# Four pairs of column groups of two up projections with tokens on partitions, most of their pairs of rows with seven block products, and the residual restored earlier

## The chip, the cores and the metric

The kernel runs on one core of a Trainium2 chip. Times are device microseconds (us) of one execution. Engines work in parallel, each in its own order of instructions: TensorE (PE) multiplies, VectorE (DVE) and ScalarE (ACT) work on elements, GpSimd (POOL) and SyncE (SP) only issue transfers here. Semaphores hold an instruction back until what it reads is there and what it overwrites is free.

## The reference

Two layers work on 256 tokens of width 2048, in fp32. Layer 0 mixes tokens with a gated MLP, layer 1 with latent attention. After each mixer comes the part that is changed here, a gated MLP with a causal convolution of width 3 between its two projections (D_FF = 5504, 43 blocks of 128 features; `w_up` is 2048 x 11008, `w_down` 5504 x 2048, `m` is the mixer's result):

```python
def conv_ffn(x, w_up, conv_w, conv_b, w_down):
    h = x @ w_up
    C = h.shape[-1]
    h = lax.conv_general_dilated(h, conv_w[:, None, :], window_strides=(1,),
                                 padding=[(CONV_W - 1, 0)],
                                 dimension_numbers=('NWC', 'WIO', 'NWC'),
                                 feature_group_count=C) + conv_b
    a, g = jnp.split(h, 2, axis=-1)
    return (jax.nn.silu(g) * a) @ w_down
...
        x = layer_norm(ALPHA * x + m, ln_mix_g[i], ln_mix_b[i])
        f = conv_ffn(x, ffn_w_up[i], ffn_conv_w[i], ffn_conv_b[i], ffn_w_down[i])
        x = layer_norm(ALPHA * x + f, ln_ffn_g[i], ln_ffn_b[i])
```

## The kernel before, in words

**Weights.** All weights stream once from memory in chunks of mostly 1 MB (128 x 2048 fp32). SP loads each into one of 3 "raw" slots. fp32 is emulated with two parts of fewer bits: ACT casts the chunk to a high part `wh` (L125), DVE subtracts that from it to get a low part `wl` (L128), each into one of 14 "big" slots. PE then multiplies three times with parts of the activations, high by high, low by high, high by low (all recorded on L230, the helper `mm`). `Feed.next` hands out chunk i, after it has issued splits up to chunk i+2 and loads up to i+4.

**Two kinds of product.** A chunk "wide" holds two k-rows of 128 by 1024 columns. With the two blocks of 128 tokens that is a product of 2x2 by 2x2 blocks: `Banks.eight` makes its eight block products, 24 matmuls of 128x512. `Banks.seven` makes it with seven products of sums of blocks, 21 matmuls; each seven chunk has its weights' sums made by DVE (`_seven`, L135: one add of 1024 elements, two of 512) and split in turn (`th` by ACT, `tl` by DVE, beside `wh` and `wl` of 1536), takes five big slots, and needs sums of the activations, made by DVE and split as well. The eight accumulators fill all eight PSUM banks; `rest` then combines four of them, and four more adds close the group. The gMLP's two projections and the down projections work like this.

**The up projection** works differently. Its 86 chunks per layer (144 to 229 in layer 0, 314 to 399 in layer 1) make groups `gi` of four chunks, 22 in all; group 0 is done with tokens on partitions at the boundary before, while the norm is still being applied. In groups 1 to 21, `prod_a` puts features on partitions: weights stand still and 512 columns move (256 tokens, high and low parts side by side), then 256 for the low part of the weights. So a group has 64 matmuls of 128x512 and 64 of 128x256 into four banks, two blocks of 128 features for `a` and two for `g`. `pair` ends a group: for each block `sum_halves` (L386 ACT copy `lo`, L388 DVE add `h`), the convolution (ACT, then two DVE scalar_tensor_tensor, L908 and L910), `silu` on ACT, and the gate's multiply (`act`, L925, DVE).

**Beside it** run three other things. `restore(f)` (L652, L653) brings back the residual, f = 0 to 3, with 4 DVE operations of 512 each and two row transfers by SP, after groups 2 to 5; `park(b)` then stores the residual by POOL after groups 4 and 6. `park_all` works on eight seven-chunks of the down projection ahead of time, 32 steps a layer, of which the groups from 2 on take up to two each: POOL loads `praw`, ACT and DVE split it and its sums (L152, L166, L167), POOL stores the four parts (L157), and they are fetched (`fwh`, `fwl`, `fth`, `ftl`, L187) when the down projection is within five chunks of their use. `acts.make` makes the first activation sums of the down projection in groups 19 and 20.

**Order.** Python code issues operations in program order, but a scheduler at build time sets the order of instructions on each engine, by what it holds ready first; on the chip each engine keeps that order.

Of the kernel before, what the change touches and what calls it, by code (L numbers as in the profile page):

```python
# [8 lines left out]
F32 = mybir.dt.float32  # L9
F32R = mybir.dt.float32r  # L10
# [5 lines left out]
P = 128  # L16
# [34 lines left out]

U_PAIRS = [[0, 1, 5, 7, 2, 6, 3, 4]] + [[0, 1, 2, 5, 3, 7, 4, 6]] * 5
U_SEVEN = [(2, 3)] + [(2, 3, 4)] * 4 + [(2, 3)]

T1, T2 = 6, 5
SLOTS = {"big": 14, "raw": 3, "side": 6}
# [15 lines left out]
def plan(n_k):  # L72

    return [[(int(t[:-1]), KINDS[t[-1]]) for t in line.split()] for line in PLAN[n_k]]
# [135 lines left out]
def trunk(ctx: ExitStack, tc: tile.TileContext, x, xT, gm_in, gm_wout, ffn_up, ffn_dn,  # L210
# [12 lines left out]
    def slot(shape, name, dt=F32, tag="big"):  # L223
        return big.tile(shape, dt, tag=tag, name=name, bufs=SLOTS[tag])
# [30 lines left out]
    def back(w, n_k):  # L255

        for hf, units in enumerate(plan(n_k)):
            c = slice(hf * 1024, (hf + 1) * 1024)
            for u, kind in units:
                if 2 * u + 1 == n_k:  # L260
                    chunks.append((w[2 * u, :, c], 1024, kind))
                    continue
                if kind == "parked":
                    parked.append(len(chunks))
                chunks.append((w[2 * u : 2 * u + 2, :, c].rearrange("k p c -> p k c"), 2048, kind))

    back(gm_wout, NF_GM)
    chunks += [(ffn_up[0, i], 2048, "") for i in range(n_up)]
    back(ffn_dn[0], NF_FF)
    chunks += [(ml_q[i], 2048, "") for i in range(4)]  # L270
    chunks += [(ml_kv[i], 3 * KVR, "") for i in range(5)] + [(ml_kv[5, :, 0:KVR], KVR, "")]
    chunks += [(ml_b[i], 2048, "") for i in range(ml_b.shape[0])]
    chunks += [(ml_out[i], 2048, "") for i in range(ml_out.shape[0])]
    chunks += [(ffn_up[1, i], 2048, "") for i in range(n_up)]
    back(ffn_dn[1], NF_FF)


# [18 lines left out]
    def combine(name, o, k1, k2):  # L296


        t = tp.tile([P, 4, P], F32, tag="t2", name=f"xs{name}", bufs=T2)
        turn(t, k1, k2)  # L300
        o = o.rearrange("p (h s c) -> p h s c", h=2, s=4)
        nc.scalar.copy(o[:, 0], t)
        nc.vector.tensor_tensor(o[:, 1], t, o[:, 0].bitcast(F32), ALU.subtract)
        return [(o[:, 0, i], o[:, 1, i]) for i in (1, 2, 0, 3)]
# [556 lines left out]
    def park_all(until):  # L861

        for i in [i for i in parked if feed.used < i < until]:
            yield from feed.park(i)
            yield
# [48 lines left out]
    def ffn(layer, ln, acc, end, last):  # L914
        act = [None] * 6
        acts = Acts(act, f"dn{layer}", NF_FF)

        def pair(a, acc_a, acc_g):
            if act[a // 8] is None:
                act[a // 8] = slot([P, 8, S], f"act{layer}_{a // 8}", tag="side" if a // 8 > 3 else "big")  # L920
            ca = conv(layer, a, acc_a, f"{layer}a{a}")
            cg = conv(layer, NF_FF + a, acc_g, f"{layer}g{a}")
            s = tp.tile([P, S], F32, tag="t1", name=f"s{layer}_{a}", bufs=T1)
            nc.scalar.activation(s, cg, AF.Silu)
            nc.vector.tensor_tensor(act[a // 8][:, a % 8, :], s, ca, ALU.mult)  # L925

        hb, ht = [], [None, None]

        def after(b, step, acc):
            if step == 0:  # L930
                ht[b] = tp.tile([P, 512], F32, tag="t2", name=f"upt{layer}_{b}", bufs=T2)
                nc.scalar.copy(ht[b], acc)
                return
            if b == 0:
                hb.extend(bank(f"uph{layer}_{f}") for f in range(2))
            for f in range(4):
                o = (f % 2) * S + b * P
                nc.tensor.transpose(hb[f // 2][:, o : o + P], ht[b][:, f * P : (f + 1) * P], ident)

        boundary(ln, acc, end, f"upf{layer}_", after)  # L940
        xhl, old = ln.new, ln
        jobs = park_all(feed.used + 2 * n_up)
        for gi in range(1, 22):
            nt, nk = (4, 4) if gi < 21 else (2, 8)
            acc = [bank(f"up{layer}_{gi}_{f}") for f in range(nt)]
            for c in range(KD // nk):
                hi, lo = feed.next()
                prod_a(acc, xhl, range(nk * c, nk * c + nk), hi, lo)
                if gi > 1 and c in (1, 2) and gi + c > 3:
                    next(jobs, None)  # L950
                if (gi, c) in FIRST:
                    acts.make(*plan(NF_FF)[0][FIRST.index((gi, c))])
                if gi == 1 and c == 0:
                    after(1, 1, None)
                    for f in range(2):
                        pair(f, hb[0][:, f * S : (f + 1) * S], hb[1][:, f * S : (f + 1) * S])
            for f in range(nt // 2):
                pair(2 * gi + f, acc[f], acc[nt // 2 + f])
            if 1 < gi < 6:
                old.restore(gi - 2)  # L960
            if gi in (4, 6):
                old.park(gi // 2 - 2)
        ln = Norm(2 * layer + 1, {}, old.put_away, last)
        return (ln, *down(NF_FF, act, f"dn{layer}", ln, acts, 4 if last else SKEW))

# [386 lines left out]
```

## Time and profile before

| what | us |
|---|---|
| median of 3 runs | 2465.73 |
| lowest and highest run | 2465.49, 2466.3 |
| profiled execution, first to last instruction (span) | 2464.6 |
| PE busy in it | 2458.1 (100%) |
| DVE busy in it | 2054.7 (83%) |
| ACT busy in it | 1459.3 (59%) |
| mean granted TensorE clock | 1.000 |

The profile records one execution; its own time is the span of 2464.6 us, and the median of the runs is 1.1 us above it. In a row such as `L128 DVE TENSOR_TENSOR wl<-raw,wh 128x1024 ... x420 | 504.1, 1220 | 86.0 <-ACT wh L125 65.3`, L128 is the line, then come engine and operation, output and inputs by the program's names, size, count, busy time in us, mean in ns of one, and the idle time of the engine right before such instructions with what ended most of it. PEld is PE's loading of weights, which goes on beside its multiplying.

### The profile page before, as it was taken

Reading aid. Unit: us, or ns where it says so; the run is one execution under the profiler, and the core shown is the slowest. Engines: PE = TensorE matmul, PEld = TensorE weight load, DVE = VectorE, ACT = ScalarE, POOL = GpSimd, SP = SyncE. Lnnn points to the kernel's source line nnn. Section 1 sums busy time; section 2 is a strip of 40 time slices with the busy share of each in tenths; the row PEclk is TensorE's granted clock in tenths of the full one; section 3 lists DMA queues with packets and bytes.
Section 4 is the critical chain, followed back from the end, with each engine's and each line's share of the span. In section 5 each row is a group of like instructions: output and inputs, shape, how many; then the busy total and the mean of one; then the engine's idle time right before and its main releaser. Section 6 shows DMA issues by size and latency. Waiting matters only on the chain. (4 is left out here: it accounts for less than half of the span.)

```text
span 2464.6 us, 32483 instructions
## 1 busy us (share of the span) xinstructions
PE 2458.1 (100%) x12494; PEld 2091.3 (85%) x12494; DVE 2054.7 (83%) x2734; ACT 1459.3 (59%) x1967; POOL 104.2 (4%) x202
## 2 busy tenths in 40 slices
PE   9999999999999999999999999999999999999999
PEld 7888888888888888888888888988888888888887
DVE  7999999989897788778777997867598787878798
ACT  6666665566565666656554566665565665555453
POOL 0000000000000000000001000000000000000000
PEclk9999999999999999999999999999999999999999
DMA  7555666656665778778868885544478787777885
GB/s 291 202 208 205 226 204 202 205 188 205 222 212 198 241 282 314 300 279 300 322 218 318 301 301 182 184 170 156 172 269 309 275 305 304 295 265 278 299 324 201
DMA packets 116428, 611.94 MB, mean 248 GB/s; under 512 B 10648, under 2 KB 10912, under 8 KB 75184
## 3 DMA queue, kind: packets, MB, share of 16 engines
q1 hardware_dynamic: 90128, 462.47, 52.9%
q0 software_dynamic: 26144, 147.39, 15.8%
q8 instruction: 98, 1.61, 0.3%
q14 instruction: 58, 0.48, 0.1%
HBM read 544.75 MB, written 65.06 MB: 247 GB/s over the span
## 5 line engine op out<-in xcount | busy, mean ns | idle before, releaser
L128 DVE TENSOR_TENSOR wl<-raw,wh 128x1024 fp32r<-128x1024 f32 (+4 forms) x645 | 958.4, 1501 | 169.5 <-ACT wh L125 124.0
L125 ACT CAST wh<-raw 128x1024 fp32r<-128x1024 f32 (+4 forms) x645 | 809.0, 1278 | 356.8 <-PE up L230 80.7
L230 PE MATMUL up<-xhl,wh 128*128 128x512 f32 x2624 | 611.4, 390 | 0.0
L230 PEld LDWEIGHTS up<-xhl,wh 128*128 128x128 f32 x2624 | 487.4, 188 | 97.8
L230 PEld LDWEIGHTS up<-xhl,wl 128*128 128x128 f32 x2624 | 325.8, 192 | 6.4
L230 PE MATMUL up<-xhl,wl 128*128 128x256 f32 x2624 | 328.1, 283 | 0.0
L125 ACT CAST th<-ts 128x1536 fp32r<-128x1536 f32 (+1 forms) x138 | 142.5, 1052 | 110.9 <-DVE ts L135 80.3
L230 PE MATMUL ub<-wh,xhl 128*128 128x512 f32 x576 | 179.5, 393 | 0.0
L128 DVE TENSOR_TENSOR tl<-ts,th 128x1536 fp32r<-128x1536 f32 (+1 forms) x138 | 163.2, 1221 | 10.4 <-PE dn_p L230 3.4
L230 PEld LDWEIGHTS ub<-wh,xhl 128*128 128x128 f32 x576 | 108.1, 188 | 24.2 <-issue 1.9
L230 PE MATMUL ub<-wl,xhl 128*128 128x512 f32 x288 | 112.1, 389 | 0.0
L135 DVE TENSOR_TENSOR ts<-ts,raw 128x512 f32<-128x512 f32 x138 | 95.1, 689 | 1.4
L135 DVE TENSOR_TENSOR ts<-raw 128x1024 f32<-128x1024 f32 x69 | 84.3, 1221 | 6.1 <-PE ub L230 3.8
L230 PE MATMUL mo<-wh,oT 128*128 128x512 f32 x256 | 82.5, 401 | 0.0
L230 PE MATMUL v_q<-wh,xhl 128*128 128x512 f32 x224 | 70.7, 391 | 0.3 <-ACT wh L125 0.3
L230 PEld LDWEIGHTS ub<-wl,xhl 128*128 128x128 f32 x288 | 54.1, 188 | 11.3
L230 PE MATMUL v_p<-wh,xhl 128*128 128x512 f32 x192 | 59.9, 389 | 0.0
L230 PEld LDWEIGHTS mo<-wh,oT 128*128 128x128 f32 x256 | 45.5, 189 | 7.1
L230 PEld LDWEIGHTS v_q<-wh,xhl 128*128 128x128 f32 x224 | 42.0, 188 | 10.5 <-ACT wh L125 1.9
L230 PE MATMUL mo<-wl,oT 128*128 128x512 f32 x128 | 50.1, 391 | 0.0
L724 ACT ACTIVATE lny<-lnt,lncol 128x128 f32<-128x128 f32 x96 | 36.6, 472 | 15.6 <-PE lnt L720 15.5
L388 DVE TENSOR_TENSOR h_0a<-up,lo_0a 128x256 f32<-128x256 f32 x41 | 17.2, 421 | 33.0 <-ACT lo_0a L386 33.0
(1838 smaller groups left out, 4338.4 us busy)
## 6 DMA issues: line engine op xcount, KB each, us to landing
raw<-in_ffn_up_dram SPq DMA_DIRECT2D x172, 1024.0 KB, 7.0
raw<-in_gm_in_dram SPq DMA_DIRECT2D x93, 1024.0 KB, 5.3
raw<-in_ffn_dn_dram SPq DMA_DIRECT2D x68, 1024.0 KB, 7.2
raw<-in_gm_wout_dram SPq DMA_DIRECT2D x48, 1024.0 KB, 5.3
praw<-in_ffn_dn_dram POOLq DMA_DIRECT2D x16, 1024.0 KB, 13.9
keptth<-pth POOLq DMA_DIRECT2D x16, 1024.0 KB, 8.1
kepttl<-ptl POOLq DMA_DIRECT2D x16, 1024.0 KB, 8.8
fth<-keptth POOLq DMA_DIRECT2D x16, 1024.0 KB, 9.4
```

The source lines that it names most:

```text
L125: cast = self.nc.scalar.copy(hi, raw)
L128: self.nc.vector.tensor_tensor(lo, raw, hi.bitcast(F32), ALU.subtract)
L135: add = lambda o, a, b: self.nc.vector.tensor_tensor(o, a, b, ALU.add)
L230: recent[0] = nc.tensor.matmul(o, l, r, start=start, stop=stop, skip_group_check=True)
L388: nc.vector.tensor_tensor(h, acc[:, 0:S], lo, ALU.add)
L724: nc.scalar.activation(y[:, j], t[:, j * P : (j + 1) * P], AF.Identity, bias=lncol[:, o : o + 1], scale=lncol[:, g : g + 1])
```

## The change

Groups 4 and 5 of each layer together, and groups 7 and 8, become a `token_group`: eight chunks, each a pair of k-rows by 512 columns of group gi and 512 of group gi+1, with tokens on partitions and all eight banks. Of the eight pairs of k, five (2, 3, 4, 5, 7) use seven products and three use eight. The activation sums for the five pairs are made in groups 2 and 3 (`sum_acts`: an add of 512, four of 128, a cast by ACT, a subtraction of 512). The result has tokens on partitions, so 16 transposes (`turn_group`) in the first chunk of the next group turn it, and `gate_group` runs `pair` on it in that group's next two chunks; there `sum_halves` is not needed, because high and low are already added. All four restores now follow groups 1 and 2, and the residual is parked after groups 2 and 3. A token group takes two parking steps, where the two groups that it replaces took four. The number of chunks and of bytes stays the same, and lines below the new code have higher numbers (L128 is L132 now, L157 L161, L187 L191, L388 L405); a token group's chunks are read as two pieces of 1024 columns instead of one of 2048.

**DVE, splitting chunks 161 and 162 of layer 0** (`wl`, `wh`, `raw`: parts of the chunk in the name; `ts`, `tl`: sums and their low part; `praw`: a parked chunk; `h_0a`, `c_0`, `act0`: the gate's tiles). Before:

```order
L128 TENSOR_TENSOR wl161_6634<-raw161_6547,wh161_6633 128x1024
L910 SCALAR_TENSOR_TENSOR c_0g5_6482<-h_0g5_6480,cst_176,c_0g5_6482 128x254
L128 TENSOR_TENSOR wl161_6634<-raw161_6547,wh161_6633 128x1024
L128 TENSOR_TENSOR wl162_6724<-raw162_6595,wh162_6723 128x1024
L925 TENSOR_TENSOR act0_0_6104<-s0_5_6486,c_0a5_6474 128x256
L128 TENSOR_TENSOR wl162_6724<-raw162_6595,wh162_6723 128x1024
```

Now, from the end of chunk 160 to the end of chunk 161 alone:

```order
L132 TENSOR_TENSOR wl160_6664<-raw160_6562,wh160_6663 128x2048
L156 TENSOR_TENSOR praw231_6444<-praw231_6444 128x512
L139 TENSOR_TENSOR ts161_6705<-raw161_6611 128x1024
L156 TENSOR_TENSOR praw231_6444<-praw231_6444 128x512
L139 TENSOR_TENSOR ts161_6705<-ts161_6705,raw161_6611 128x512
L156 TENSOR_TENSOR praw231_6444<-praw231_6444 128x512
L132 TENSOR_TENSOR wl161_6707<-raw161_6611,wh161_6706 128x1536
L156 TENSOR_TENSOR praw231_6444<-praw231_6444 128x512
L139 TENSOR_TENSOR ts161_6705<-ts161_6705,raw161_6611 128x512
L132 TENSOR_TENSOR tl161_6709<-ts161_6705,th161_6708 128x1536
L132 TENSOR_TENSOR tl161_6709<-ts161_6705,th161_6708 128x512
L405 TENSOR_TENSOR h_0a6_6755<-up0_3_0_6552,lo_0a6_6753 128x256
```

Two casts a chunk became six instructions for a seven, and four sums of a parked chunk stand between them.

**DVE, chunks 157 to 159, in group 2** (`res`: residual, `lnp`: its rows, `xr`, `xs`: activation sums). Before:

```order
L128 TENSOR_TENSOR wl157_6412<-raw157_6335,wh157_6411 128x1024 x2
L653 TENSOR_TENSOR res0_1_5507<-res0_1_5507,lnp0_21_6934 128x512 x2
L652 TENSOR_TENSOR res0_1_5507<-res0_1_5507,lnp0_30_7156 128x512
L128 TENSOR_TENSOR wl158_6502<-raw158_6375,wh158_6501 128x1024 x2
L653 TENSOR_TENSOR res0_1_5507<-res0_1_5507,lnp0_31_7158 128x512
L652 TENSOR_TENSOR res0_1_5507<-res0_1_5507,lnp0_30_7156 128x512
L128 TENSOR_TENSOR wl159_6542<-raw159_6417,wh159_6541 128x1024
L388 TENSOR_TENSOR h_0a4_6453<-up0_2_0_6285,lo_0a4_6451 128x256
```

Now:

```order
L309 TENSOR_TENSOR xs0_4_6449<-xr0_4_6447 128x128
L132 TENSOR_TENSOR wl157_6457<-raw157_6361,wh157_6456 128x1024
L310 TENSOR_TENSOR xs0_4_6449<-xs0_4_6449,xr0_4_6447 128x128
L132 TENSOR_TENSOR wl158_6557<-raw158_6410,wh158_6556 128x1024
L311 TENSOR_TENSOR xs0_4_6449<-xr0_4_6447,xs0_4_6449 128x128
L405 TENSOR_TENSOR h_0a4_6498<-up0_2_0_6301,lo_0a4_6496 128x256
L669 TENSOR_TENSOR res0_1_5507<-res0_1_5507,lnp0_20_6534 128x512 x2
L320 TENSOR_TENSOR xs0_4_6446<-xs0_4_6449,xs0_4_6446 128x512
L925 SCALAR_TENSOR_TENSOR c_0a4_6500<-h_0a4_6498,cst_176,c_0a4_6500 128x255
L405 TENSOR_TENSOR h_0g4_6506<-up0_2_2_6303,lo_0g4_6504 128x256
```

The sums stand between the casts of chunks 157 and 158.

**PE, the third seven of the first token group, chunk 163** (`upt0_4_q5` and so on: the accumulators). Before, its group 4 read, for chunk 161:

```order
L230 MATMUL up0_4_0_6719<-xhl1_1_5783,wl161_6634 128x256
L230 MATMUL up0_4_1_6720<-xhl1_1_5783,wl161_6634 128x256
L230 MATMUL up0_4_2_6721<-xhl1_1_5783,wl161_6634 128x256
L230 MATMUL up0_4_3_6722<-xhl1_1_5783,wl161_6634 128x256
```

Now, at the end of chunk 163:

```order
L234 MATMUL upt0_4_p7_6799<-th163_6852,xs0_4_6446 128x512 x2
L234 MATMUL upt0_4_q4_6796<-th163_6852,xhl1_2_5784 128x512 x2
L234 MATMUL upt0_4_p6_6800<-th163_6852,xs0_4_6446 128x512 x2
L234 MATMUL upt0_4_q5_6798<-tl163_6853,xs0_4_6446 128x512
L234 MATMUL upt0_4_p7_6799<-tl163_6853,xs0_4_6446 128x512
L234 MATMUL upt0_4_p6_6800<-tl163_6853,xs0_4_6446 128x512
L234 MATMUL upt0_4_q4_6796<-tl163_6853,xhl1_2_5784 128x512
L234 MATMUL upt0_4_q3_6793<-wh164_6886,xhl1_0_5782 128x512 x2
```

The products with `tl` come last in a seven; the next chunk follows them directly.

**POOL, end of parking in layer 0** (`kept`: stores; `f`: fetches). Before:

```order
L157 DMA keptth266_9813<-pth266_9809 128x2048
L157 DMA kepttl266_9815<-ptl266_9810 128x2048
L187 DMA fwh231_10242<-keptwh231_6585 128x1536
L187 DMA fwl231_10244<-keptwl231_6587 128x1536
L187 DMA fth231_10246<-keptth231_6807 128x2048
L187 DMA ftl231_10248<-kepttl231_6809 128x2048
```

Now:

```order
L161 DMA keptth266_10192<-pth266_10188 128x2048
L191 DMA fwh231_10204<-keptwh231_6649 128x1536
L161 DMA kepttl266_10194<-ptl266_10189 128x2048
L191 DMA fwl231_10206<-keptwl231_6651 128x1536
L191 DMA fth231_10208<-keptth231_6845 128x2048
L191 DMA ftl231_10210<-kepttl231_6847 128x2048
```

The order is nearly the same; the stores for chunk 266 belong to a step that was in group 18 and is now in group 20.

```diff
--- before.py
+++ after.py
@@ -52,6 +52,10 @@
 U_PAIRS = [[0, 1, 5, 7, 2, 6, 3, 4]] + [[0, 1, 2, 5, 3, 7, 4, 6]] * 5
 U_SEVEN = [(2, 3)] + [(2, 3, 4)] * 4 + [(2, 3)]
 
+UP_TOKEN = (4, 7)
+UP_PAIRS = (0, 2, 3, 4, 1, 5, 7, 6)
+UP_SEVEN = (2, 3, 4, 5, 7)
+
 T1, T2 = 6, 5
 SLOTS = {"big": 14, "raw": 3, "side": 6}
 
@@ -264,14 +268,27 @@
                     parked.append(len(chunks))
                 chunks.append((w[2 * u : 2 * u + 2, :, c].rearrange("k p c -> p k c"), 2048, kind))
 
+    def up(layer):
+
+        for gi in range(22):
+            if gi - 1 in UP_TOKEN:
+                continue
+            if gi not in UP_TOKEN:
+                chunks.extend((ffn_up[layer, i], 2048, "") for i in range(4 * gi, min(4 * gi + 4, n_up)))
+                continue
+            for p in UP_PAIRS:
+                i = 4 * gi + p // 2
+                w = ffn_up[layer, i : i + 5 : 4, :, p % 2 * 1024 : p % 2 * 1024 + 1024].rearrange("f p c -> p f c")
+                chunks.append((w, 2048, "seven" if p in UP_SEVEN else "wide"))
+
     back(gm_wout, NF_GM)
-    chunks += [(ffn_up[0, i], 2048, "") for i in range(n_up)]
+    up(0)
     back(ffn_dn[0], NF_FF)
     chunks += [(ml_q[i], 2048, "") for i in range(4)]
     chunks += [(ml_kv[i], 3 * KVR, "") for i in range(5)] + [(ml_kv[5, :, 0:KVR], KVR, "")]
     chunks += [(ml_b[i], 2048, "") for i in range(ml_b.shape[0])]
     chunks += [(ml_out[i], 2048, "") for i in range(ml_out.shape[0])]
-    chunks += [(ffn_up[1, i], 2048, "") for i in range(n_up)]
+    up(1)
     back(ffn_dn[1], NF_FF)
 
 
@@ -940,7 +957,61 @@
         boundary(ln, acc, end, f"upf{layer}_", after)
         xhl, old = ln.new, ln
         jobs = park_all(feed.used + 2 * n_up)
+        sums, rooms, turning = {}, [], []
+
+        def sum_acts(p):
+
+            if len(sums) % 2 == 0:
+                rooms.append(slot([P, 2, 8 * P], f"xs{layer}_{p}", F32R, "side" if len(rooms) < 2 else "big"))
+            t = xhl[p // 2][:, 2 * (p % 2) : 2 * (p % 2) + 2]
+            raw = tp.tile([P, 2, S], F32, tag="t2", name=f"xr{layer}_{p}", bufs=T2)
+            nc.vector.tensor_tensor(raw, t[:, :, 0:S].bitcast(F32), t[:, :, S : 2 * S].bitcast(F32), ALU.add)
+            sums[p] = combine(f"{layer}_{p}", rooms[-1][:, len(sums) % 2, :], raw[:, 0], raw[:, 1])
+
+        def token_group(gi):
+
+            acc = Banks(f"upt{layer}_{gi}", DIRECT + OWN)
+            for c, p in enumerate(UP_PAIRS):
+                a = [[x_parts(xhl, 2 * p + j, b) for j in range(2)] for b in range(2)]
+                got = feed.next()
+                if p in UP_SEVEN:
+                    acc.seven(a, sums[p], *got, turned=512, across=True)
+                    if p == [q for q in UP_PAIRS if q in UP_SEVEN][-1]:
+                        rest = acc.rest()
+                else:
+                    acc.eight(a, *got, across=True)
+                if c in (0, 7):
+                    next(jobs, None)
+                yield
+            for n, t in zip(DIRECT, rest):
+                nc.vector.tensor_tensor(t, acc.acc[n], t, ALU.add)
+            turning.append((gi, rest, [bank(f"upr{layer}_{gi}_{i}") for i in range(4)]))
+
+        def turn_group():
+
+            gi, rest, t = turning[0]
+            for i, r in enumerate(rest):
+                b, f = i // 2, i % 2
+                for j in range(4):
+                    o = (j % 2) * S + b * P
+                    nc.tensor.transpose(t[2 * f + j // 2][:, o : o + P], r[:, j * P : (j + 1) * P], ident)
+
+        def gate_group(f):
+
+            gi, rest, t = turning[0]
+            for j in range(2):
+                c = slice(j * S, (j + 1) * S)
+                pair(2 * (gi + f) + j, t[2 * f][:, c], t[2 * f + 1][:, c])
+            if f == 1:
+                turning.pop()
+
         for gi in range(1, 22):
+            if gi - 1 in UP_TOKEN:
+                continue
+            if gi in UP_TOKEN:
+                for _ in token_group(gi):
+                    pass
+                continue
             nt, nk = (4, 4) if gi < 21 else (2, 8)
             acc = [bank(f"up{layer}_{gi}_{f}") for f in range(nt)]
             for c in range(KD // nk):
@@ -950,16 +1021,23 @@
                     next(jobs, None)
                 if (gi, c) in FIRST:
                     acts.make(*plan(NF_FF)[0][FIRST.index((gi, c))])
+                if turning and c == 0:
+                    turn_group()
+                if turning and c in (1, 2):
+                    gate_group(c - 1)
+                if gi in (2, 3) and c < 3 and len(sums) < len(UP_SEVEN):
+                    sum_acts(UP_SEVEN[len(sums)])
                 if gi == 1 and c == 0:
                     after(1, 1, None)
                     for f in range(2):
                         pair(f, hb[0][:, f * S : (f + 1) * S], hb[1][:, f * S : (f + 1) * S])
             for f in range(nt // 2):
                 pair(2 * gi + f, acc[f], acc[nt // 2 + f])
-            if 1 < gi < 6:
-                old.restore(gi - 2)
-            if gi in (4, 6):
-                old.park(gi // 2 - 2)
+            if gi < 3:
+                old.restore(2 * gi - 2)
+                old.restore(2 * gi - 1)
+            if gi in (2, 3):
+                old.park(gi - 2)
         ln = Norm(2 * layer + 1, {}, old.put_away, last)
         return (ln, *down(NF_FF, act, f"dn{layer}", ln, acts, 4 if last else SKEW))
```

## The prediction

> **What bounds the kernel now.** First the page's first part, then the chain of waits, then windows over the stage that is changed (up projection of layer 0: 810 to 1260; of layer 1: 1782 to 2232) and over three stretches where VectorE (DVE) is loaded most.
>
> ```profile
> PE 2458.1 (100%) x12494; PEld 2091.3 (85%) x12494; DVE 2054.7 (83%) x2734; ACT 1459.3 (59%) x1967; POOL 104.2 (4%) x202
> ```
>
> Columns of the windows: from:to, length, then busy time (and count) of PE, PEld, DVE, ACT and POOL, granted clock, DMA share, GB/s.
>
> ```profile
> 810.00:1260.00 450.00, 450.00 (x2588) 398.03 (x2587) 357.85 (x514) 269.93 (x385) 25.41 (x45) 1.00 0.77 287
> 1782.00:2232.00 450.00, 450.00 (x2594) 398.60 (x2593) 361.02 (x519) 270.93 (x386) 25.45 (x45) 1.00 0.77 286
> 833.00:855.00 22.00, 22.00 (x129) 19.45 (x128) 21.38 (x34) 11.89 (x18) 0.57 (x1) 1.00 0.86 269
> 111.00:152.00 41.00, 41.00 (x183) 33.94 (x182) 39.81 (x37) 27.48 (x34) 0.00 (x0) 1.00 0.59 208
> 373.00:421.00 48.00, 48.00 (x219) 39.35 (x218) 44.23 (x45) 27.72 (x30) 2.15 (x4) 1.00 0.61 197
> 421.00:469.00 48.00, 48.00 (x214) 38.67 (x213) 44.36 (x45) 28.52 (x28) 2.14 (x4) 1.00 0.64 201
> ```
>
> In the up stage PE is busy in every microsecond at full clock, so a product saved there is time saved, as long as nothing else falls behind. DVE has 80% of the stage on average (358 of 450), but 21.38 of 22.00 where restores lie (833 to 855). That stretch is the one that the change loads.
>
> **PE's side: what is saved.** Three rows of the chain:
>
> ```profile
> 1607.64 0.87 PE qrt L1093 x8
> 1782.32 450.10 PE up L230 x2592
> 2233.77 1.36 PE dn_p L230 x6
> ```
>
> A group before is 128 matmuls, so 450.10 × 128/2592 = 22.23 us, and two groups 44.46. A token group has 3 chunks of 24 and 5 of 21 products of 128x512, 177, at 1.36/6 = 0.2267: 40.1. It adds 16 transposes at 0.87/8 = 0.109: 1.7. Net −2.6 a token group, −10.4 for all four, if PE never waits.
>
> **DVE's side: what is added.**
>
> ```profile
> L128 DVE TENSOR_TENSOR wl<-raw,wh 128x1024 fp32r<-128x1024 f32 x420 | 504.1, 1220 | 86.0 <-ACT wh L125 65.3 <-issue 10.4 <-PE up L230 8.2
> L128 DVE TENSOR_TENSOR wl<-raw,wh 128x2048 fp32r<-128x2048 f32 x140 | 319.4, 2290 | 74.0 <-ACT wh L125 55.6 <-PE dn_q L230 13.8 <-issue 2.1
> L128 DVE TENSOR_TENSOR tl<-ts,th 128x1536 fp32r<-128x1536 f32 x69 | 121.1, 1755 | 10.4 <-PE dn_p L230 3.4 <-ACT th L125 3.4 <-PE v_p L230 1.9
> L135 DVE TENSOR_TENSOR ts<-raw 128x1024 f32<-128x1024 f32 x69 | 84.3, 1221 | 6.1 <-PE ub L230 3.8 <-DMA raw<-in_gm_in_dram 0.9 <-PE wo_q L230 0.7
> L135 DVE TENSOR_TENSOR ts<-ts,raw 128x512 f32<-128x512 f32 x138 | 95.1, 689 | 1.4
> L908 DVE SCALAR_TENSOR_TENSOR c_0a<-h_0a,cst,c_0a 128x255 f32<-128x255 f32 x41 | 19.7, 480 | 9.3 <-ACT c_0a L907 9.2
> L388 DVE TENSOR_TENSOR h_0a<-up,lo_0a 128x256 f32<-128x256 f32 x41 | 17.2, 421 | 33.0 <-ACT lo_0a L386 33.0
> L294 DVE TENSOR_TENSOR xs<-xraw,xs 128x128 f32<-128x128 f32 x4 | 1.2, 292 | 0.1
> ```
>
> The timeline of DVE, at the start of the stage in each layer and over a seven-product chunk of the mixer:
>
> ```profile
> 139.95 1.22 DVE L135 TENSOR_TENSOR ts<-raw 128x1024 f32<-128x1024 f32 x1
> 141.21 1.42 DVE L135 TENSOR_TENSOR ts<-ts,raw 128x512 f32<-128x512 f32 x2
> 142.54 1.75 DVE L128 TENSOR_TENSOR wl<-raw,wh 128x1536 fp32r<-128x1536 f32 x1
> 144.21 2.35 DVE L128 TENSOR_TENSOR tl<-ts,th 128x1536 fp32r<-128x1536 f32 x2
> 146.66 2.29 DVE L128 TENSOR_TENSOR wl<-raw,wh 128x2048 fp32r<-128x2048 f32 x1
> ...
> 829.32 5.76 DVE L128 TENSOR_TENSOR wl<-raw,wh 128x1024 fp32r<-128x1024 f32 x5
> 835.00 1.29 DVE L652 TENSOR_TENSOR res<-res,lnp 128x512 f32<-128x512 f32 x2
> ...
> 1789.91 5.76 DVE L128 TENSOR_TENSOR wl<-raw,wh 128x1024 fp32r<-128x1024 f32 x5
> ```
>
> Five casts of 1.22 fill 5.76: instructions overlap by 0.08, so one costs its duration less 0.08. By element count: 1.14 (1024), 2.21 (2048), 1.67 (1536), 0.60 (512), 0.34 (256), 0.40 (the convolutions' scalar_tensor_tensor), 0.21 (128). A seven then costs DVE 1.14 + 2×0.60 + 2×1.67 + 0.60 = 6.28 (6.71 by the timeline, 139.95 to 146.66, waits included), where an ordinary chunk costs 2.27. PE needs 21×0.2267 = 4.76 for a seven. So within token groups DVE needs more than PE, and only a lead can hide it.
>
> I walk both DVE orders from a point that they share, the last cast of chunk 153 (in layer 1, chunk 323), which ends at 835.00 before; call it T = 0. Up to the last low part of chunk 179, where the second token group ends, DVE now has, per layer: 20 casts of 1024 (22.7), 10 sevens (62.8), 6 wide casts (13.2), 16 restore steps (9.6), 48 convolution steps (19.0), 16 half sums h (5.4), 12 gates (4.1), parking (8 adds, 2 tl, 2 wl: 12.6), five activation sums (0.60 + 4×0.21 + 0.60 each: 10.1) and 8 adds that close the first token group (4.8). That is 164.4 us. The same walk of the old order gives 117.5: 52 casts of 1024 (59.1) stand for sevens and wide casts, and there are no sums.
>
> ```profile
> L386 ACT COPY lo_0a<-up x41: 347/357/377, 837.8 to 1275.4; 128x256 f32<-128x256 f32 x41
> ```
>
> PE begins group 2 at T = 2.5 (first half-copy of group 1 at 837.8) and ended chunk 179, seven groups on, at 2.5 + 7×22.23 = 158.0. Unstalled it would now be there at 2.5 + 3×22.23 + 2×40.1 + 1.7 = 151.1. But DVE finishes that chunk's weights only at 164.4 with no idle time at all; 16 of the chunk's 24 products remain after them (3.6), so PE ends at 168.0, and the second 16 transposes add 1.7: 169.7, or 11.7 later than before. The lead is spent early: at chunk 163, DVE's tl comes at T = 76.3, while PE unstalled would begin that chunk at 61.9. Groups 2 and 3 hold the five sums and the restores that used to spread to group 5, so the cover is gone before the first seven.
>
> DVE is never quite without idle time. In its fullest stretches 2.8% (833 to 855) and 2.9% (111 to 152) were idle, in the two windows of the u projection, which has sevens too, 7.7% ((96 − 88.59)/96). On 164 that is 4.7 to 12.6. The 6.71 against 6.28 of the seven adds 0.43 on ten of them, 4.3, in the same place; I take 6, close to the low end because the walk has no slack where DVE could wait for PE. Per layer 11.7 + 6 = 17.7, for both 35.4. Nothing is won back later: after group 9 PE is again the bound, at 22.23 a group.
>
> **What costs nothing more.**
>
> ```profile
> L125 ACT CAST th<-ts 128x1536 fp32r<-128x1536 f32 x69 | 102.4, 1484 | 91.5 <-DVE ts L135 61.0 <-PE dn_q L230 13.1 <-PE v_q L230 8.6
> L653 DVE TENSOR_TENSOR res<-res,lnp 128x512 f32<-128x512 f32 x24 | 16.0, 685 | 0.2 <-DMA lnp<-in_ln_rows_dram 0.2
> ```
>
> ACT's cast of 1536 (1.48) is shorter than DVE's subtraction of the same size (1.75), ACT has none of the three adds beside them, and it stands at 270 of 450: it hides behind DVE. Chunks arrive as 4 KB pieces instead of 8 KB; the share of 0.77 leaves room, and slower PE and DVE ask for less per microsecond. If transfers did become late, it would show as DMA waits before casts; from 0 to 2 us, I take 0. Restoring sooner shifts 16 steps of 0.60 forward inside the same stage and is in the walk. SP issues the same chunks; the rows for restores (DVE waited 0.2 for them in all) go out up to two groups sooner and share five buffers with the sums' raw tiles and the closing tiles. Behind a late one would stand DVE's next casts, and PE behind those; the idle time of 6 has to hold that. POOL issues parking later, and that has a deadline:
>
> ```profile
> 1203.19 0.53 POOL L157 DMA_DIRECT2D keptth<-pth  x1 [18.98 <-ACT pth L166]
> 1211.57 0.53 POOL L187 DMA_DIRECT2D ftl<-kepttl  x1 [3.64 <-DMA keptth<-pth]
> ...
> ftl<-kepttl POOLq DMA_DIRECT2D x2, 1024.0 KB, 17.7
> ...
> 1277.16 0.62 PE L230 MATMUL dn_q<-fwh,dn01px 128*128 128x512 f32 x2
> ```
>
> The last parking step moves from group 18 to group 20, eight chunks of 22.23/4, or 44.5 later relative to the stage's end. ftl would be issued at 1211.57 + 44.5 = 1256.1, land 17.7 later at 1273.8, and is first wanted 2 to 3 us after 1277.16. About 3.4 us is left to the first use of its group: cost 0 if that holds, up to about 5 us a layer if the fetches queue.
>
> **The sum.** Span 2464.6 + 35.4 = 2500.0. The median of the runs stands 1.1 above the span (2465.73): 2501, and I say **2500**.
>
> **Rivals.** *Cover holds, faster.* DVE's lead at T = 0 is longer than the walk has it, or PE's saving arrives whole: 2465.7 − 10.4 = 2455. For it: PE at 100% kernel-wide against DVE at 83%, and 54 us more a layer (sevens 40.1, sums 10.1, closing adds 9.6, fewer h −5.4, wide casts −0.4) would still leave DVE at 2054.7 + 108 = 2163, 88% of the time. Against it: 164.4 against 151.1 at one place, where the average says nothing. The Trainium skill, page "Perfetto Trace Analysis", section "Identifying the Most-Contended Engine", says to optimise the engine with the highest occupancy first; by that rule this change is the right way round. The same page, under "Optimization Strategy", warns that the most-contended engine can change between regimes, and the 21.38 of 22.00 above agrees with the warning.
>
> *DVE idles as in the u projection, slower still.* There sevens alternate with wide chunks and DVE lost 7.7%; with 12.6 a layer: 2 × (11.7 + 12.6) = 48.6, so 2514. For it: sevens, closing adds and parking take turns on two engines here too. Against it: PE was the bound there and DVE waited for its slots; here PE is behind.
>
> *Parking late.* The sum of the main case and 5 us a layer: 2510. It decides from a margin of 3.4 us that any stall of POOL eats.
>
> *The sevens overlap better than rows say.* If DVE reaches its walk with no idle time and the prices are 2.5% too dear (4 a layer): 2465.7 + 2 × 7.7 = 2481.
>
> **How the numbers follow.** Main case 0.62, DVE idling more 0.15, parking late 0.13, cover holding 0.07, no change that can be measured 0.02; the remaining 0.01 is for slower by other ways. A measurement of this kernel tells 0.2%, about 5 us, from no change. Faster is 0.07, same 0.02, slower 0.91. The range, 2481 to 2518, reaches from the cheap walk to the idle one with a part of the parking, and leaves out the case in which the cover holds.
>
> **What would show it.** In the changed trace: PE idle for the first time in the up stage, in groups 4 to 8 (about 881 to 1010 and 1842 to 1970), with DVE tl or wl as what ended it, some 23 us a layer (169.7 + 6 against 151.1 + 1.7); DVE 95% busy or more from 835 to 1005; the stage near 450 + 18; 22.23 a group from group 10 on; other stages unchanged. Wrong if PE waits for ACT, DMA or banks there, if DVE has over 8% idle in that stretch, if PE first waits outside it, or if fetched parts are what it waits for after 1277.

## The result, and the profile after

The changed kernel takes 2501.24 us (2500.2 to 2501.59), the kernel before 2465.61 in the same session: a ratio of 1.0144, 95% interval 1.0131 to 1.0156, slower by 35.6 us. The forecast was 2500. The profiled execution has a span of 2498.4 us, 33.8 more than before, and is compared here.

The page's first part, after:

```profile
PE 2468.8 (99%) x12242; PEld 2073.8 (83%) x12242; DVE 2158.7 (86%) x2862; ACT 1484.2 (59%) x1957; POOL 104.2 (4%) x202
```

DVE has 104.0 us more than before (108 were forecast) and is still, over the whole kernel, less busy than PE. What matters stands in the windows over the up stage of layer 0 (columns as in the prediction):

```profile
833.00:855.00 22.00, 22.00 (x129) 19.46 (x128) 21.87 (x42) 11.87 (x19) 1.26 (x2) 1.00 0.85 311
855.00:881.00 26.00, 26.00 (x151) 23.03 (x151) 25.16 (x48) 12.99 (x21) 1.63 (x3) 1.00 0.86 284
881.00:925.00 44.00, 37.63 (x142) 26.30 (x141) 42.78 (x49) 25.44 (x27) 1.77 (x3) 0.96 0.64 228
925.00:970.00 45.00, 43.92 (x229) 36.62 (x227) 43.59 (x57) 26.66 (x34) 1.09 (x2) 1.00 0.63 222
970.00:1005.00 35.00, 32.21 (x124) 23.27 (x125) 34.70 (x39) 22.99 (x25) 1.77 (x3) 0.95 0.68 240
1030.00:1260.00 230.00, 230.00 (x1326) 203.64 (x1325) 187.67 (x269) 143.13 (x206) 14.33 (x25) 1.00 0.78 291
```

In this stage PE is idle in groups 4 to 8 only (881 to 1005), 10.2 us, and never from 1030 to 1260. DVE is busy 168.1 of the 172 us from 833 to 1005. What PE waited for between 800 and 1100 (us in total, times, longest):

```profile
PE upt_q L234 <- DVE tl L132: 3.4, 6, 0.9
PE upt_q L234 <- ACT th L129: 2.1, 4, 1.1
PE upt_q L234 <- DVE wl L132: 1.7, 3, 1.1
PE upt_p L234 <- DVE h_0g L405: 1.4, 1, 1.4
PE upt_p L234 <- DVE h_0a L405: 0.4, 2, 0.2
PE upt_e L234 <- DVE c_0a L927: 0.3, 1, 0.3
PE upt_q L234 <- ACT wh L129: 0.3, 1, 0.3
```

These are 18 waits, 9.6 us in all. Of them 5.1 end with a low part by DVE (`tl`, `wl`), 2.4 with a cast by ACT, and 2.1 with a step of the gate by DVE (`h`, `c`), which by the program is the last reader of a bank that a token group's product writes next.

The timeline of DVE has the shared point (last cast of chunk 153) and the last low part of chunk 179, the first of the three casts in the last row:

```profile
828.72 5.76 DVE L132 TENSOR_TENSOR wl<-raw,wh 128x1024 fp32r<-128x1024 f32 x5
834.40 1.29 DVE L669 TENSOR_TENSOR res<-res,lnp 128x512 f32<-128x512 f32 x2
...
1001.87 4.56 DVE L132 TENSOR_TENSOR wl<-raw,wh 128x2048 fp32r<-128x2048 f32 x3 [0.23 <-ACT wh L129]
```

T = 0 is 834.40. A cast of 2048 from 1001.87 ends at about 1004.1 (2.2 by the prediction's price), T = 169.7; the walk with its idle time had 164.4 + 6 = 170.4.

**Group by group.** The table gives PE's time from the first product of a token group to its last, less the few ordinary products between, from the timelines; the ideal is the count of products times 0.2267.

| kernel | ideal | layer 0 | layer 1 |
|---|---|---|---|
| changed | 40.1 | 52.1, 49.2 | 52.2, 49.3 |
| sums left out | 40.1 | 42.5, 49.3 | 43.4, 49.3 |
| eight products only | 43.5 | 43.5, 43.5 | 43.5, 43.5 |
| three sevens, same places | 41.5 | 45.2, 43.7 | 48.2, 43.7 |
| five sevens, groups 8 and 13 | 40.1 | 43.4, 51.0 | 43.9, 51.3 |
| four sevens, 6 and 11, the change's parking | 40.8 | 42.5, 47.7 | 42.4, 48.6 |
| three sevens, 6 and 11 | 41.5 | 41.8, 44.8 | 41.7, 45.4 |
| three sevens, 6 alone | 41.5 | 41.7 | 41.7 |
| restores late | 40.1 | 49.7, 55.1 | 50.3, 55.4 |
| only the storing late | 40.1 | 52.1, 49.2 | 52.3, 49.1 |

In the change 12.0 + 9.1 = 21.1 us are lost in layer 0 (22.9 were forecast). Three terms make up most of it. The listed waits: 9.6. A slower clock (last section): 3.4. And, as an estimate, what a wait hides: a row of PE is drawn 0.39 long where the next product starts 0.23 later, so listed idle time begins 0.16 late, and the first product after it is drawn 0.50 long, 0.11 more. These 0.27 for each of the 18 waits listed are 4.9. The remaining 3.2 are gaps too short to be listed and small differences between products.

### The profile page after: what moved, and what is told of

Read it like the earlier page. It is cut to its first block, busy times and chain, and to the rows that moved or that the text cites. A ratio compares the mean times of both kernels' runs of the same rounds, so it can differ in the third digit from the quotient of the medians.

```text
span 2498.4 us, 32131 instructions
## 1 busy us (share of the span) xinstructions
PE 2468.8 (99%) x12242; PEld 2073.8 (83%) x12242; DVE 2158.7 (86%) x2862; ACT 1484.2 (59%) x1957; POOL 104.2 (4%) x202
## 5 line engine op out<-in xcount | busy, mean ns | idle before, releaser
L132 DVE TENSOR_TENSOR wl<-raw,wh 128x1024 fp32r<-128x1024 f32 (+5 forms) x613 | 942.3, 1555 | 142.2 <-ACT wh L129 107.4
L129 ACT CAST wh<-raw 128x1024 fp32r<-128x1024 f32 (+5 forms) x613 | 794.2, 1320 | 340.6 <-PE up L234 66.4
L234 PE MATMUL up<-xhl,wh 128*128 128x512 f32 x2112 | 493.6, 390 | 0.0
L234 PEld LDWEIGHTS up<-xhl,wh 128*128 128x128 f32 x2112 | 392.3, 188 | 78.7
L129 ACT CAST th<-ts 128x1536 fp32r<-128x1536 f32 (+1 forms) x178 | 184.6, 1051 | 151.3 <-DVE ts L139 127.2
L234 PEld LDWEIGHTS up<-xhl,wl 128*128 128x128 f32 x2112 | 262.4, 192 | 5.1
L234 PE MATMUL up<-xhl,wl 128*128 128x256 f32 x2112 | 265.1, 283 | 0.0
L132 DVE TENSOR_TENSOR tl<-ts,th 128x1536 fp32r<-128x1536 f32 (+1 forms) x178 | 210.8, 1222 | 9.7 <-PE dn_p L234 3.4
L139 DVE TENSOR_TENSOR ts<-ts,raw 128x512 f32<-128x512 f32 x178 | 122.8, 690 | 1.9
L234 PEld LDWEIGHTS mo<-wh,oT 128*128 128x128 f32 x256 | 45.4, 189 | 7.2
L741 ACT ACTIVATE lny<-lnt,lncol 128x128 f32<-128x128 f32 x96 | 36.6, 472 | 15.6 <-PE lnt L737 15.5
L156 DVE TENSOR_TENSOR praw<-praw 128x512 f32<-128x512 f32 x64 | 44.1, 689 | 0.7
```

The lines of the kernel that those rows point to most:

```text
L129: cast = self.nc.scalar.copy(hi, raw)
L132: self.nc.vector.tensor_tensor(lo, raw, hi.bitcast(F32), ALU.subtract)
L139: add = lambda o, a, b: self.nc.vector.tensor_tensor(o, a, b, ALU.add)
L156: add = lambda o, a, b: pin(nc.vector.tensor_tensor(o, a, b, ALU.add))
L234: recent[0] = nc.tensor.matmul(o, l, r, start=start, stop=stop, skip_group_check=True)
L741: nc.scalar.activation(y[:, j], t[:, j * P : (j + 1) * P], AF.Identity, bias=lncol[:, o : o + 1], scale=lncol[:, g : g + 1])
```

## The experiments

**Leaving out the sums.**

```diff
-                    sum_acts(UP_SEVEN[len(sums)])
+                    p = UP_SEVEN[len(sums)]
+                    sums[p] = [x_parts(xhl, 2 * p + j, b) for j in range(2) for b in range(2)]
```

> The changed kernel with the five activation sums of each layer left out (the seven products read ordinary blocks of the activations in their place, so that the result is not the reference's); products, token groups, weights' sums and restores stay. Theory (VectorE is late from groups 2 and 3 on, and each microsecond of its work before chunk 179 comes back as time): the sums are 10.1 us of VectorE per layer, so 20 us of the 35.6 go away: about 2481. Rival (PE stalls because of the form of the token groups themselves: banks, restarts of PE after each short wait, clock): the sums are not its cause, and the time stays at 2496 to 2501.

Measured 2481.14, 20.1 us less than the change: as much as the sums cost DVE comes back. Nearly all of it comes back in the first token group of each layer (52.1 to 42.5 and 52.2 to 43.4); the second loses as much as before. With the sums go five casts by ACT and one of the 14 big slots, which this run doesn't separate from DVE's work.

**No token groups, all the rest.**

```diff
-UP_TOKEN = (4, 7)
+UP_TOKEN = ()
```

> The changed kernel without any token group: all groups as before, but the five activation sums per layer are made (and not used) in groups 2 and 3, and restores and parking of the residual come as early as in the change. Theory: VectorE's 20 us of additional or earlier work in groups 2 and 3 are just covered by its lead (its walk has the last low part of chunk 160 at 48.3 us, PE begins that chunk at 46.9 and wants low parts last): 2466 to 2469. Rival (the early restores and the sums are by themselves what costs): 2475 or more.

Measured 2466.05, ratio 1.000 (0.9991 to 1.001). Sums and early restores are hidden where nothing follows that wants DVE more than PE.

**Eight products only.**

```diff
-UP_SEVEN = (2, 3, 4, 5, 7)
+UP_SEVEN = ()
...
-            acc = Banks(f"upt{layer}_{gi}", DIRECT + OWN)
+            acc = Banks(f"upt{layer}_{gi}", DIRECT)
...
-            for n, t in zip(DIRECT, rest):
-                nc.vector.tensor_tensor(t, acc.acc[n], t, ALU.add)
+            rest = []
+            for n in DIRECT:
+                rest.append(tp.tile([P, 512], F32, tag="t2", name=f"upt{layer}_{gi}r{n}", bufs=T2))
+                nc.scalar.copy(rest[-1], acc.acc[n])
```

> The changed kernel with token groups of eight products only: no sums of weights or activations, ScalarE copies the four banks before they are turned. Theory (sevens cost VectorE 6.28 us where PE saves 0.68, everything else in the form is cheap): PE does 8 x 24 products of 0.2267 and 16 transposes, 45.3 us instead of 44.46, VectorE does less than before, so 4 x 0.8 = 3 us slower than before, 2469, without idle PE in groups 4 to 8. Rival (the form stalls PE by itself: banks, transposes, 4 KB pieces): PE idle there, 2475 or more.

Measured 2471.65, ratio 1.0025 (1.0015 to 1.0034); 2.8 above the sum, of which 2.0 are PE's waits at the start of the two down projections. Its windows:

```profile
875.00:925.00 50.00, 50.00 (x238) 42.03 (x237) 31.70 (x35) 25.08 (x28) 1.76 (x3) 1.00 0.75 274
925.00:975.00 50.00, 50.00 (x260) 43.02 (x259) 38.88 (x50) 30.16 (x36) 2.86 (x5) 1.00 0.76 281
```

PE is never idle here, and DVE is busy 31.70 of 50. So transposes and 4 KB pieces stall nothing; the sevens do, with what belongs to them. This kernel also leaves out the activation sums and the four banks that only sevens use, so it is no test of the banks; in the change, 2.1 of the 9.6 us of waits are for banks.

**Later places.**

```diff
-UP_TOKEN = (4, 7)
+UP_TOKEN = (8, 13)
...
-                if gi in (2, 3) and c < 3 and len(sums) < len(UP_SEVEN):
+                if gi in (5, 6) and c < 3 and len(sums) < len(UP_SEVEN):
```

> The changed kernel with its token groups at column groups 8 and 13 instead of 4 and 7, and the activation sums in groups 5 and 6 instead of 2 and 3; the same operations in all. Theory: groups 2 and 3 hold only restores, VectorE has its full lead (about two chunks, some 10 us) at the start of each token group and has time to win it back between them; it needs 52 us for eight chunks of a token group where PE needs 40, so 2 to 6 us are lost in each instead of 10, against 4.3 less products and 1.7 more transposes: 2465 to 2486, about 2475. Rival (a token group loses its 10 us wherever it stands, because a seven costs VectorE more than PE): 2496 to 2502.

Measured 2486.82: better than the change by 14, and just above the expected range. In layer 0 the group at 8 loses 3.3, the one at 13 loses 10.9. In the latter PE's longest wait is 2.99 us (for wl), and ACT waited for PE, a row that the change hardly has. From the timelines of PE and of ACT in that group:

```profile
1105.39 0.79 PE L234 MATMUL upt_q<-wl,xs 128*128 128x512 f32 x1 [2.99 <-DVE wl L132]
```

```profile
1111.65 1.49 ACT L129 CAST wh<-raw 128x1536 fp32r<-128x1536 f32 x1 [2.21 <-PE upt_p L234]
1117.16 2.00 ACT L129 CAST th<-ts 128x1536 fp32r<-128x1536 f32 x2 [4.02 <-PE upt_q L234]
```

By the program, a cast that waits for a product waits for the slot that the product reads. By group 13 four tiles of gates and one of sums hold five of the 14 slots, and a seven takes five.

**Three sevens at the same places.**

```diff
-UP_SEVEN = (2, 3, 4, 5, 7)
+UP_SEVEN = (2, 3, 5)
```

> The changed kernel, token groups at the same places and the same order of pairs, but three of eight pairs (2, 3, 5) with seven products and three activation sums. Theory (VectorE's work decides, a seven costs it 4.0 us more than two casts and a sum 2.0): 4 sevens and 2 sums less are 20 us less per layer before chunk 179; its walk then has chunk 162 at 60.8 us where PE wants it at 60.3, and chunk 179 at 144.0 where PE is there at 150, so about 1 to 2 us are lost per layer. PE does 183 products and 16 transposes, 43.2 us instead of 44.46, 4.9 us less for four groups, and up to 2 us are lost at the start of the down projection as in the other runs: 2463 to 2469. Rival (restarts and the form cost as much as the sevens): 2480 or more.

Measured 2476.21, better than the change by 25 but above the expectation: PE lost 5.9 and 8.9 us in the layers' token groups, not 1 to 2 (the profiled execution took 2480.31, 4 above the median). The expectation had left out the idle allowance of 6 us a layer that the prediction used; DVE was idle 5.8 us from 835 to 1005 here, and with that allowance the sum is about right.

**Groups 6 and 11, four and five sevens, parking in threes.**

```diff
-UP_TOKEN = (4, 7)
-UP_PAIRS = (0, 2, 3, 4, 1, 5, 7, 6)
-UP_SEVEN = (2, 3, 4, 5, 7)
+UP_TOKEN = (6, 11)
+UP_PAIRS = (0, 2, 1, 3, 4, 7, 5, 6)
+UP_SEVEN = (2, 3, 4, 5)
...
-                if c in (0, 7):
-                    next(jobs, None)
...
-                if gi > 1 and c in (1, 2) and gi + c > 3:
+                if gi > 1 and c > 0 and gi + c > 3 and not turning:
```

The sums move to groups 3 and 4. With five sevens the pairs are 2, 3, 4, 5, 7 in the order 0, 2, 3, 1, 4, 5, 7, 6.

> Token groups at column groups 6 and 11, four of eight pairs (2 to 5) with seven products, alternating with the others, activation sums two each in groups 3 and 4, and the steps of parking taken out of the token groups and the group behind each, three a group elsewhere. Theory: VectorE is never more than its lead behind; its walk has the last seven's low part of the first token group about when PE begins that chunk. PE does 180 products and 16 transposes, 42.5 us instead of 44.46, 7.6 less for four groups; 0 to 2 us lost at the start of the down projection, up to 5 in waits: 2457 to 2465. Rival (slots: later token groups wait for slots whatever VectorE does, as the second one at group 13 did): 2470 or more.

> As the run with four sevens at groups 6 and 11, but with the changed kernel's five pairs with seven products (2, 3, 4, 5, 7), in the order 0, 2, 3, 1, 4, 5, 7, 6; five sums in groups 3 and 4. Theory: PE does 177 products, 10.4 us less for four groups than before; VectorE does 6 us more in each token group than with four, and two or three sevens in a row want more slots than there are: 2456 if it just holds, 2468 if each token group loses 3 us. Rival (slots): 2475 or more.

Measured 2490.48 and 2518.87: both far off, in the range of the rivals, but for a reason that neither theory nor rival had. PE now waits in ordinary groups. In the run with five, ACT's timeline shows why:

```profile
890.07 0.60 ACT L924 ACTIVATE c_0g<-h_0g,cst 128x256 f32<-128x256 f32 x1
899.65 1.48 ACT L170 CAST pwh<-praw 128x1536 fp32r<-128x1536 f32 x1 [8.98 <-DMA praw<-in_ffn_dn_dram]
```

Over the whole of that run (busy, mean ns, idle time before it):

```profile
L170 ACT CAST pwh<-praw 128x1536 fp32r<-128x1536 f32 x16 | 23.7, 1479 | 58.0 <-DMA praw<-in_ffn_dn_dram 58.0
```

With a step in each chunk, the parked chunk's cast comes one chunk (5.6 us) after its load is issued, which takes 14.0 (median of that run), and all casts behind it on ACT wait. The row has 44.2 us of such idle time in the run with four sevens, and had 7.9 before.

**The same with the change's parking, four and three sevens.** Parking again after the second and third chunk of ordinary groups, in token groups after the third and seventh; with three sevens the pairs are 2, 3, 5 in the order 0, 2, 1, 3, 4, 5, 6, 7.

```diff
-                if c in (0, 7):
+                if c in (2, 6):
                     next(jobs, None)
```

> As the run with four sevens at groups 6 and 11, but with the steps of parking as in the change (two a group, two in a token group, at its third and seventh chunk), so that a parked chunk's cast never follows its load by less than three chunks. Theory: the losses of that run in ordinary groups (ScalarE held by the cast of a parked chunk whose load had not landed) are gone; four sevens alternating with wide chunks lose 2 to 4 us in a token group by waits and restarts, against 1.9 saved: 2464 to 2472. Rival (slots make any later token group wait): 2478 or more.

> As the run with four sevens at groups 6 and 11 and parking as in the change, with three sevens (2, 3, 5) between single wide chunks. Theory: VectorE needs 4 us less per token group and never two sevens in a row, so PE waits for nothing in the token groups; 4.9 us less products than before, up to 2 lost at the start of the down projection: 2461 to 2465. Rival (slots, or short waits with restarts): 2468 or more.

Measured 2488.98 (1.0093) and 2471.04 (1.0022, 1.0013 to 1.0031). The parked cast's stall is gone, but both times are in the rivals' ranges, the second 6 us above what was expected. With four, the group at 11 loses 7 to 8 us, and behind each token group ordinary products wait for `rest` to clear the banks (upt_6w and upt_11w, 0.8 to 1.2 a time). With three, the group at 6 is free of loss, the group at 11 loses 3 to 4.

**Restores late, and only the storing late.**

```diff
-            if gi < 3:
-                old.restore(2 * gi - 2)
-                old.restore(2 * gi - 1)
-            if gi in (2, 3):
-                old.park(gi - 2)
+            if 8 < gi < 13:
+                old.restore(gi - 9)
+            if gi in (11, 13):
+                old.park(gi // 2 - 5)
```

The second leaves the restores early and moves only the two `park` lines.

> The changed kernel with the four restores after groups 9 to 12 and the residual parked after groups 11 and 13, everything else as in the change. Theory in its plain form (only VectorE's work before chunk 179 counts): 16 steps of 0.60 leave the stretch, VectorE's walk has chunk 163 at 59.4 us instead of 76.3 and chunk 179 at 147.4 instead of 164.4, PE unstalled needs 61.9 and 151.1, so the loss shrinks from 21 us a layer to 3 to 6, and the time is 2463 to 2470. Rival (slots: the residual keeps two of the 14 big slots through both token groups, a seven takes five; splits then wait for PE to free slots whatever VectorE does): 2480 or more, with ScalarE's casts waiting for PE in the token groups.

> The changed kernel with nothing moved but the storing of the residual, after groups 11 and 13 instead of 2 and 3; the restores stay early and VectorE's order is the same instruction by instruction. The residual then keeps two of the 14 big slots through both token groups. Theory (the late restores of the run before lost their time to slots): casts wait for PE to free slots, and 5 us or more a layer come on top of VectorE's lateness, 2508 or more. Rival (VectorE's lateness alone sets the time, since casts that come sooner than VectorE can use them are worth nothing): 2499 to 2503 as in the change; the late restores then lost their time by their place in VectorE's order.

Measured 2507.86 for the first (17 us less of DVE work before chunk 179 by the walk, and yet slower than the change) and 2501.73 for the second, the change's time. In the first, DVE is busy 148.4 of the 170 us from 835 to 1005, where the change has 166.1: the work went away and came back as idle time. (The 16 restore steps make only 9.6 of the 17; what the rest is was not taken apart.) Waits of ACT from 881 to 1008 in the first:

```profile
ACT wh L129 <- PE upt_p L234: 8.1, 5, 3.3
ACT th L129 <- PE upt_q L234: 4.4, 2, 4.0
```

The change has 1.5 us of such waits there. That fits slots that bind once DVE is early enough to want them, and cost nothing while DVE is late.

It leaves 6 us between the two: with the same two slots taken, the kernel with less to do is the slower one. In its DVE order the previous group's gates stand between two parts of the first seven, where they wait for that group's end; but the token group in which this happens is the shorter one (49.7 against 52.1). The loss is in the second token groups (55.1 against 49.2, 55.4 against 49.1). There PE's waits are longer (up to 2.7 us in layer 0, for `wl`, against 1.4), and the clock falls further: from 957 to 1013 the granted clock is 0.91 with PE busy 48.3 us, while the second run has 1.00 in its own second group. That is an estimated 4 of the 5.9 us in layer 0 (0.09 of 48.3); in layer 1 the clocks differ less (0.94 from 1939 to 1996 against 0.97 from 1939 to 1990). Why the waits are longer, by slots or by order, was not separated.

**One token group, three sevens.** The last variant with a token group at 6 alone.

```diff
-UP_TOKEN = (6, 11)
+UP_TOKEN = (6,)
```

> One token group per layer only, at column group 6, three sevens (2, 3, 5) between wide chunks, sums in groups 3 and 4. In the run with two such groups PE stood idle nowhere in the first one in either layer. Theory (a token group that VectorE covers saves what its products save): 183 products of 0.2267 and 16 transposes against 44.46 are 1.2 us less per layer, with parking ending a group earlier so that the down projection begins without a wait: 2463 to 2464.5, the only version below the kernel before, by less than 0.2%. Rival (unlisted short waits and restarts take as much as the products save): 2465 to 2470.

Measured 2463.67 (2462.99 to 2464.14), ratio 0.9992, 0.9983 to 1.0001: as the sum has it (41.7 + 1.7 − 44.46 = −1.1 a layer), but not clear of no change.

## Why the prediction was right

- **PE's saving** (−2.6 a token group): right. Where PE waits for nothing, a token group takes its ideal time: 43.5 against 43.5 with eight products, 41.7 against 41.5 with three sevens.
- **DVE's walk** (164.4 us; 169.7 measured with idle time, 165.8 without): right for the change's order, so the prices were not too dear either. That this work is the cause is shown by leaving out 10 us of it (20.1 us back for two layers) and by leaving out the sevens with all that belongs to them (PE idle nowhere in the token groups). It is no rule for other orders: with the restores taken out of the stretch, nothing came back.
- **DVE's idle time** (6 a layer): 3.9 us from 833 to 1005. PE's last product of the second token group ended at T = 173.8, where the walk with its idle time had 174.0. That the token groups lose 21.1, and not the 22.9 forecast, is mostly that PE came to the first one at T = 48.0 and not at 47.0.
- **Its own signs of being wrong** named waits of PE for ACT or banks, and there were such waits: 2.4 and 2.1 of the 9.6 us. ACT's casts of `th` had themselves waited for DVE's `ts` (24.5 us from 881 to 1008), and the steps that free the banks are DVE's. So DVE's lateness reaches PE in three ways, of which the prediction had one.
- **Per layer** 17.7 forecast. The same ordinary products open layer 1's up stage in both chains of waits, before and after:

```profile
1777.47 4.41 PE up L230 x27
```

```profile
1795.04 4.41 PE up L234 x27
```

  Layer 0 has cost 17.6 by then, 15.5 of it by the first product of the down projection (1287.27 against 1271.72) and the rest after it; layer 1 adds the other 16.2 of the span's 33.8. So some of the closeness to 2500 is luck: the up stage cost about 2 us less than forecast, and the down projection of layer 0 about 2 more. Nothing is won back, as forecast: from 1030 to 1260 PE is busy in all 230 us.
- **Parking late** (0.13): no fetched part was waited for; ftl was issued 22 us before its first use, about as forecast:

```profile
1272.98 0.53 POOL L191 DMA_DIRECT2D ftl<-kepttl  x1 [0.93 <-DMA keptth<-pth]
```

```profile
1295.20 0.39 PE L234 MATMUL dn_q<-ftl,dn01px 128*128 128x512 f32 x1
```

  Still the later stores and fetches cost something that the prediction had at nothing. They now share the transfer engines with the first loads of the down projection. Windows of 50 us at its start, before and after:

```profile
1245.00:1295.00 50.00, 50.00 (x256) 42.83 (x255) 41.63 (x68) 30.49 (x42) 2.11 (x4) 1.00 0.66 233
```

```profile
1260.00:1310.00 50.00, 48.53 (x249) 41.05 (x249) 40.29 (x62) 30.45 (x41) 5.34 (x10) 1.00 0.91 336
```

  The share of DMA went from 0.66 to 0.91, and ACT and PE waited:

```profile
1286.35 1.91 ACT L129 CAST wh<-raw 128x2048 fp32r<-128x2048 f32 x1 [3.84 <-DMA raw<-in_ffn_dn_dram]
```

```profile
1296.79 0.74 PE L234 MATMUL dn_p<-fth,dn01px 128*128 128x512 f32 x2 [0.52 <-DVE h_0a L405]
1298.72 0.73 PE L234 MATMUL dn_p<-fth,dn01px 128*128 128x512 f32 x2 [0.95 <-DVE h_0g L405]
```

  That is 1.5 us in layer 0 and 0.2 in layer 1. PE's two waits end with the last group's half sums by DVE, not with a transfer. Where parking ends sooner (one token group, or parking in threes), these waits are absent; that the later parking is their cause is read from the traces, not tested alone.
- **Cover holds** (0.07): did not happen. The rule that spoke for it, in the Trainium skill's "Perfetto Trace Analysis", "Identifying the Most-Contended Engine", judges TensorE by its weight loads and by its share of peak arithmetic, not by its busy matmul time. The prediction had left that out. By the weight loads TensorE came first before the change, but narrowly (85% against DVE's 83%), and after it DVE does (86% against 83%). In the window 833 to 855 before, the same measure already has DVE first, 21.38 us against 19.45.
- **Idle as in the u projection** (0.15): did not happen; DVE was busy 97.7% from 833 to 1005.
- **Slots** were set aside ("here PE is behind"). For the change that is shown (2501.73 with two less); it does not hold for versions in which DVE is early.

## What to carry to other kernels

Trading one engine's work for another's pays only where the second engine has room in that very stretch: add up its work from a point that both orders share and compare it with the time of the first engine, chunk by chunk. Cover is used up before the place that needs it: the sums, with the early restores, cost nothing by themselves, and the sums alone cost 20 us in front of the sevens. Such a reckoning holds for the order that it was made for: less work in another order did not help. A step that waits for its own transfer on an in-order engine has to keep its distance from that transfer when steps are packed closer.

## What was not expected of the hardware

The granted clock fell to half although PE never stood still for long. Two rows of PE with the waits ahead of the first fall, and windows of 2 us:

```profile
889.91 0.50 PE L234 MATMUL upt_q<-wl,xs 128*128 128x512 f32 x1 [0.38 <-DVE wl L132]
...
891.77 0.73 PE L234 MATMUL upt_q<-th,xhl 128*128 128x512 f32 x2 [1.12 <-ACT th L129]
```

```profile
890.00:892.00 2.00, 0.88 (x3) 0.44 (x4) 2.00 (x3) 0.90 (x2) 0.00 (x0) 1.00 0.00 0
892.00:894.00 2.00, 1.11 (x4) 0.53 (x4) 2.00 (x4) 1.39 (x2) 0.00 (x0) 1.00 0.72 246
894.00:896.00 2.00, 2.00 (x6) 1.54 (x6) 1.97 (x3) 0.95 (x3) 0.00 (x0) 0.51 0.68 279
896.00:898.00 2.00, 2.00 (x7) 1.38 (x6) 2.00 (x4) 1.13 (x2) 0.00 (x0) 0.64 0.00 0
```

Four microseconds in which PE was busy half the time, with no wait over 1.12, were followed by 3.4 at half clock, which costs 0.49 × 2 + 0.36 × 2 = 1.7 us; it happens once in each token group of layer 0, 3.4 in all. The share alone doesn't decide: from 904 to 908 PE was busy 2.34 of 4 us and the clock stayed at 1.00, while 2.45 of 4 from 972 to 976 were followed by the second fall. The Trainium skill, "TensorE: Matmul & The Clock Gate", Part 1, puts the fall after at least one idle window of some 3.4 us. This trace disagrees as far as "idle" means no products at all: half-busy was enough.
